# A hybrid decoder block on one core: the last unit's scores, the query remainder's buffer, and the last inverse deviation

## The chip, the cores and the metric

The kernel runs on one core of a Trainium2 chip. A core has TensorE (matrix products, "PE" in the profile, its weight loads "PEld"), VectorE ("DVE"), ScalarE ("ACT"), GpSimd ("POOL") and SyncE ("SP"), which here only issues DMAs. Each engine works through its own queue in order; the queues are tied to each other by semaphores. The metric is the time of one execution on the device in microseconds; of several runs the median is given.

## The reference

One decoder block over 512 tokens with 16 meta tokens put in front (L = 528 rows), model width 1024, in float32.

```python
h = layer_norm(concat(meta, x))
proj = h @ w_in                    # q, k, v, gate of both branches, two merge gates
# branch d: 8 heads, two score maps each, ALiBi, softmax; a = p0 - lam * p1; y_d = rms_norm(a @ v)
# branch s: 16 heads, stick-breaking:
z = q @ k.T * 64 ** -0.5
log_keep = where(before, log_sigmoid(-z), 0)
a = where(before, exp(log_sigmoid(z) + suffix_sum(log_keep)), 0)
y_s = a @ v
br_d = (y_d * silu(g_d)) @ w_br_diff
br_s = (y_s * silu(g_s)) @ w_br_sb
y = (sigmoid(m_d + b0) * br_d + sigmoid(m_s + b1) * br_s) @ w_out
out = layer_norm(2 ** 0.25 * h + y)[16:]
```

## The kernel before

**Precision.** Every large product is done in three: operands are split into a high part, rounded for the fast matmul form, and a remainder, and high times high, high times remainder and remainder times high are summed in PSUM. `hi` and `lo` (lines 176 to 192) split the weights, four blocks of 128 rows at a time ("a half"); the function `prep` does this four halves ahead of the use and fetches more weights. The remainders are subtractions on VectorE, the high parts casts on ACT.

**Units.** The attention runs in 16 units (`UNITS`): units 0 to 7 are the heads of branch d, units 8 to 15 are pairs of heads of branch s. While unit u does its scores, transposes and products with v, TensorE also projects the keys and values of unit u + 1 (`stage_kv`), the queries of unit u + 2 (`stage_q`) and a gate or two. In each unit the projections are generators that yield a time after each small step, and the function `run` (line 571) drives them; it holds a list of (time, work) pairs, the steps, and puts each piece of work out when the sum of the yielded times has passed its time. So the step times set the order in which instructions are written.

**What sets the order on the engines.** The written order is not yet the order of the queues. A planner simulates the program on a timeline at build time and draws up each engine's queue; it takes instructions that its simulation holds ready, earlier written ones first, and gives each tile one of the buffers of its ring as they come free. Where the kernel wants its own order it adds dependencies that need no semaphore: `keep_order` (line 235) ties each instruction of an engine to the one written before it. This is done for everything before the units, for all engines and SP from line 1027 on (the branch products, the output projection, the last LayerNorm), and, for TensorE alone, from a marker in the last unit on: the step at `LAST[0][0] - 0.1` (line 1022) stores the position, and line 1225 ties TensorE's instructions from there. Instructions written before the marker are free.

**A unit of branch s.** `s_scores` (line 892) does one head c of the pair: for the four blocks of 128 queries, from the last to the first, one or two score tiles (widths 264 and 264, 400, 272, 144), each two matmuls into a bank of the two called "sc" (line 756), two sigmoids on ACT (lines 902 and 904) which free that bank, then a scan and a product on VectorE (lines 908 and 909) which write the block of the weights a into the padded tile `apad`. It is a generator with five steps. `transposed` gives three parts that turn `apad` block by block on TensorE (line 768) into a bank of the two called "tp", and split what was turned (lines 773 and 774). `s_values` multiplies with v (lines 917 to 925) into the bank "av", and copies the result out (lines 929 to 933). `values` (line 720) prepares v: it turns vT into two "tp" banks, tv and t4, and splits them into V and v4 (lines 745 and 746, and line 747 for the last block); V has one buffer, so these casts follow the last product of the unit before.

**The last unit** (u = 15) has no keys or queries to project. Its projections are gate d, three merge gates and gate s, eight steps of 0.64 each. The scores of head 0 are put out at 0, 0.85, ..., 3.4, those of head 1 at 4.4, 5.25, 6.1, 6.95 and 7.8; the transposes of both at the times of `LAST`: 13.0, 14.1, 18.2 (with the product with v at 21.2) and 21.9, 21.9, 23.2 (24.9).

**The query remainder.** `stage_q` (line 606) scales the projected queries on ACT into A[0], takes the remainder on VectorE into the tile `low` (line 614) and sends three half tiles on by DMA (line 616). `low` comes from the ring "sg", six buffers of 128 x 512, which also serves the gates' sigmoids, the head outputs `ys`, and the reloads `gr` and `yd` of `late_gate` (lines 547 to 549). The tag "bias" of the pool `ap` has two buffers of 128 x 528; branch d keeps its biases there, and from unit 8 on one of them holds `diag`, a row mask for the scans.

**The end.** The output projection runs in two column halves c and four row blocks t (line 1188). In the second half each row block is finished: residual (line 1197), statistics (line 1200), their aggregation (line 1205), the inverse deviation by `rstd_of` (line 296: on GpSimd, an addition and a power of -0.5), then on VectorE `shift` (line 1210, subtract the mean and multiply by the weight) and `scale` (line 1214, multiply by the inverse deviation and add the bias), and the store. For the last row block the scaling and the store are done in two halves. ACT's last work is splitting `w_out` in the first column half (line 1131) and issuing two loads (line 1196).

Of the kernel before, what the change touches and what calls it, by code (L numbers as in the profile page):

```python
# [10 lines left out]
F32R = mybir.dt.float32r  # L11
BF16 = mybir.dt.bfloat16
AF = mybir.ActivationFunctionType
# [3 lines left out]
P = 128  # L17
D = 1024
KT = D // P
S = 512  # L20
M = 16
L = M + S
# [24 lines left out]
def hybrid_block_kernel(ctx: ExitStack, tc: tile.TileContext, x, meta, emb_g, emb_b, w_in, b_gate,  # L47
                        diff_lambda, subln_g, w_br_d, w_br_s, w_out, ln_g, ln_b, out):
    nc = tc.nc
    v, s, g, pe = nc.vector, nc.scalar, nc.gpsimd, nc.tensor  # L50
# [10 lines left out]
    gpool = ctx.enter_context(tc.tile_pool(name="g", bufs=6))  # L61
# [29 lines left out]
    for n, (kind, i) in enumerate(seq):  # L91
# [17 lines left out]
        else:  # L109
            c = COL[kind] + i * P  # L110
# [168 lines left out]
    epsr = const.tile([P, 1], F32, name="epsr")  # L279
# [16 lines left out]
    def rstd_of(pool, var, rs, n):  # L296
        e = pool.tile([P, 1], F32, tag="lne", name="lne")
        g.tensor_tensor(e[:n], var, epsr[:n], op=ALU.add)
        g.tensor_tensor(rs, e[:n], neghalf[:n], op=ALU.pow)
# [149 lines left out]
    def lam2():  # L449
        v.tensor_scalar(nlam, lexp[:, 1:2], lexp[:, 0:1], -LAM_INIT, op0=ALU.subtract, op1=ALU.add)  # L450

    steps = dict(a=scaled, d=lambda b, k: scaled(b, k, v), x=lambda b, k: query(0, P * b, P, k),
                 y=lambda h, k: query(1, 256 * h, 256, k), s=lambda h, k: high(h, k, s.copy),
                 h=lambda h, k: high(h, k, v.tensor_copy), l=low, N=norms, S=stat)
# [128 lines left out]
    with tc.tile_pool(name="att", bufs=1) as ap:  # L583
# [15 lines left out]
        diag, staged = [], []  # L599
# [6 lines left out]
        def stage_q(unit, kind, n):  # L606

            res = []
            yield from proj_tok(res, "q" + kind, n)
            ps = res[0]  # L610
            A = [apool.tile([P, S], F32R, tag=f"A{c}", name=f"A{c}") for c in range(2)]
            low = gpool.tile([P, S], F32R, tag="sg", name="low")
            s.activation(A[0], ps, AF.Copy, scale=0.125)
            v.scalar_tensor_tensor(low, ps, 0.125, A[0].bitcast(F32), op0=ALU.mult, op1=ALU.subtract)  # L614
            for o, src in ((A[1][LO], A[0][HI]), (A[1][HI], low[HI]), (A[0][HI], low[LO])):
                nc.sync.dma_start(o.bitcast(F32), src.bitcast(F32))
            unit["A"] = A
            yield 0.64
# [273 lines left out]
        def s_scores(unit, c, first):  # L892
            A = unit["A"]
            a = apads[c]
            sg, om = E
            for i in reversed(range(NB)):
                nk, z0 = NKEY[i], ZOFF[i]
                for n, (ps, k0, use) in enumerate(logits(A[c], K[c], i)):
                    if n == 1:
                        yield  # L900
                    o = ds(z0 + k0, use)
                    s.activation(om[:, o], ps[:, :use], AF.Sigmoid, scale=-1.0)  # L902
                    behind("act", first)
                    s.activation(sg[:, o], ps[:, :use], AF.Sigmoid)  # L904
                    behind("act", first)

                rev = om[:, z0:z0 + nk][:, ::-1]
                v.tensor_tensor_scan(rev, rev, diag[0][:, L - nk:][:, ::-1], 0.0, ALU.mult, ALU.max)  # L908
                v.tensor_tensor(a[:, ds(AOFF[i], nk - 1)], sg[:, ds(z0, nk - 1)], om[:, ds(z0 + 1, nk - 1)],
                                op=ALU.mult)  # L910
                yield
# [29 lines left out]
        def spread(gen, t0, dt, count):  # L941
            return [(t0 + dt * m, lambda: next(gen)) for m in range(count)]
# [12 lines left out]
        for u, (kind, n) in enumerate(UNITS):  # L955
            unit = units[u]
            if u + 3 == SEVEN:
                pools["rawk"] = ap
            last = u + 1 == len(UNITS)
            proj = [] if last else keys_values(units[u + 1], *UNITS[u + 1])  # L960
            if u + 2 < len(UNITS):
                proj.append(stage_q(units[u + 2], *UNITS[u + 2]))
            steps = pending + [(0.6, lambda unit=unit: values(unit, kind))]
            pending = []
            if u + 1 < SEVEN:
                steps.append((9.2, store_k))
            if u in SUMS_AT:
                if not tS:
                    tS.append(ypool.tile([P, KT, L], F32R, tag="ys", name="tS"))
                steps += [(t, lambda k=u + (u > 1) + m: placed(lambda: input_sums(k))) for m, t in enumerate(SUMS_AT[u])]  # L970
            if u in GATE_AT and u < 14:
                proj.append(raw_gate(GATE_AT[u], kept["r"][GATE_AT[u]]))
            if kind == "d":
                ta = {}
                dt, t0, t1 = TD[u in GATE_AT]
                steps += spread(d_scores(unit, n), 0.0, dt, 10)
                parts = transposed(ta, apads[n % 2])
                steps += [(t0 + 0.7 * m, f) for m, f in enumerate(parts)]
                steps.append((t1, lambda: d_values(unit, ta)))
                pending = [(3.0 if n < 7 else 5.8, lambda unit=unit, n=n: d_norm(unit, n))]  # L980
            else:
                if n == 0:
                    diag.append(ap.tile([P, L], F32, tag="bias", name="diag", bufs=2))
                    g.memset(diag[0], 0.0)
                    g.tensor_copy(diag[0][:, L - P:], ident)
                    g.memset(v3[:, 1], 0.0)
                    for a in apads:
                        for i in range(NB):
                            g.memset(a[:, ds(AOFF[i] + NKEY[i] - 1, 1)], 0.0)
                if last:  # L990
                    ydT = [pair_of("ydT", n=S) for k in range(4)]
                    ydT = [ydT[k % 4][:, k // 4, :] for k in range(8)]
                    ysT = ypool.tile([P, 8, S], F32, tag="ys", name="ysT")
                    ysT = [ysT[:, k, :] for k in range(8)]
                    unit["y"] = ysT[7]

                    def fill_in(y, of):
                        placed(lambda: nc.sync.dma_start(y, of), [mybir.EngineType.SP])

                    fill_in(ydT[7], kept["d"][7])  # L1000
                    for m, (y, of) in enumerate(((ydT, "gd"), (ysT, "gs"))):
                        for j in range(7):
                            steps.append((1.3 + 1.5 * (7 * m + j), lambda o=y[j], x=kept[of][j]: fill_in(o, x)))
                    proj += [gate("d", n, lambda: ydT[7]), merge_gate(0, 0), merge_gate(0, 1), merge_gate(0, 2),
                             gate("s", n, lambda: ysT[7])]
                else:
                    if GATE_AT.get(u) == n:
                        yd = gpool.tile([P, S], F32, tag="sg", name="yd")
                        nc.sync.dma_start(yd, kept["d"][n])
                        proj.append(gate("d", n, lambda yd=yd: yd, kept["gd"][n]))  # L1010
                    else:
                        steps += zip((12.0, 24.0), late_gate(ap, *(kept[x][n] for x in ("d", "r", "gd"))))
                    proj.append(gate("s", n, lambda unit=unit: unit["y"], kept["gs"][n]))
                for c in range(2):
                    ta = {}
                    steps += spread(s_scores(unit, c, n == 0), (2.0 + 4.3 * c) if n == 0 else 4.4 * c, 0.85, 5)
                    parts = transposed(ta, apads[c])
                    times = LAST[c] if last else [7.0 + 6.5 * c + 0.7 * m for m in range(3)] + [10.5 + 6.5 * c]
                    steps += zip(times, parts)
                    steps.append((times[3], lambda c=c, ta=ta: s_values(unit, c, n, ta)))  # L1020
                if last:
                    steps.append((LAST[0][0] - 0.1, lambda: state.update(ends=len(nc.cur_bb.bb.instructions))))
            run(proj, steps)
# [5 lines left out]
    lr = ctx.enter_context(tc.tile_pool(name="later", bufs=2))  # L1029
# [111 lines left out]
    for p in range(4):  # L1141
        steps = []
# [16 lines left out]
    def residual(t):  # L1159
        hr = hrs[t]  # L1160
        v.scalar_tensor_tensor(hr, hr, xmv[:, t, 0:1], vec["eg"], op0=ALU.subtract, op1=ALU.mult)
        v.scalar_tensor_tensor(hr, hr, xrs[:, t:t + 1], vec["eb"], op0=ALU.mult, op1=ALU.add)
# [4 lines left out]
    for k in range(5, KT):  # L1167
        split_out(0, k)
        if k == 5:
# [4 lines left out]
    MEANWHILE = [[lambda k=k: split_out(1, k) for k in range(3)] + [lambda: residual(0), lambda: load_rows(1)],  # L1174
                 [lambda k=k: split_out(1, k) for k in range(3, 6)] + [lambda: residual(1), lambda: load_rows(2)],
                 [lambda k=k: split_out(1, k) for k in range(6, 8)] + [lambda: residual(2), lambda: load_rows(3)],
                 [lambda: residual(3)], [], [], [], []]
    for c in range(2):
        for t in range(NB):
            st, final = sts[t], t == NB - 1  # L1180
# [22 lines left out]
            mv = lr.tile([P, 2], F32, tag="fmv", name="fmv")  # L1203
            rs = lr.tile([P, 1], F32, tag="frs", name="frs")
            v.bn_aggr(mv, st[:, :4 if final else 2])
            rstd_of(lr, mv[:, 1:2], rs, P)

            def shift(o, w, t=t, mv=mv):
                a = hrs[t][:, ds(o, w)]
# [46 lines left out]
```

## Time and profile before

| | us |
|---|---|
| median of 3 runs | 708.45 (708.07 to 708.89) |
| the profiled execution | 708.69 |
| its span, first to last instruction | 706.9 |
| the units, to the start of the branch products | 541.5 |
| branch products, gates and rounding to the first output product | 113.8 |
| output projection | 44.1 |
| behind the last matmul | 7.5 |

The granted TensorE clock was 0.998 of full speed over the span. The rows of the timeline give start and duration in microseconds, engine, line, operation, output from input, and in brackets how long the engine had been idle and what released it. A wait list gives, for an engine and a line, what it waited for: the sum, how often, and the longest. Matmuls are pipelined: they start 0.23 us (512 wide) or 0.12 us (264 wide) apart while each lasts longer, so starts are to be compared, not ends.

### The profile page before, as it was taken

To read this page: it belongs to the slowest core of one execution; us is meant where nothing else is said; L and a number is where in the kernel's file an instruction comes from. 1 tells how busy PE (TensorE), PEld (TensorE's weight loads), DVE (VectorE), ACT (ScalarE), POOL (GpSimd) and SP (SyncE) were. 2 spreads that over 40 slices of the span, in tenths; PEclk is the share of its full clock that TensorE was granted. 3 is DMA by queue.
4 is the path that set the end of the run, shared out by engine and by line. 5 is a ranking of instruction groups with operands and counts; after the bars stand their busy time and mean duration, and the time that the engine had idled before them with its cause. 6 is when DMAs were issued, how large, how long until landed. Compare 5 with 4: busy or idle time off the path is not lost.

```text
span 706.9 us, 13294 instructions
## 1 busy us (share of the span) xinstructions
PE 696.0 (98%) x4482; PEld 635.9 (90%) x4482; DVE 569.5 (81%) x1224; ACT 439.3 (62%) x1068; POOL 132.9 (19%) x146
## 2 busy tenths in 40 slices
PE   9999999999999999999999999999999999999995
PEld 8999999989989898988889899988888998999885
DVE  6887998878687687989787898966665888688886
ACT  5776768757566687776767687766555456555400
POOL 3243112322222101212123020000012201230012
PEclk9999999999999999999999999999999999999999
DMA  8398557988898886899897976645576749796702
GB/s 286 104 198 179 144 121 173 216 184 178 210 195 184 198 189 175 170 218 197 210 201 180 241 150 180 178 113 179 189 179 129 153 120 235 149 178 185 266 20 115
DMA packets 184054, 124.93 MB, mean 177 GB/s; under 512 B 8961, under 2 KB 168098, under 8 KB 183986
## 3 DMA queue, kind: packets, MB, share of 16 engines
q1 hardware_dynamic: 147890, 102.84, 50.0%
q0 software_dynamic: 35776, 20.19, 22.9%
q10 hardware_dynamic: 320, 1.06, 0.4%
q8 instruction: 35, 0.57, 0.4%
q14 instruction: 33, 0.27, 0.1%
HBM read 93.54 MB, written 9.44 MB: 146 GB/s over the span
## 4 chain that ended last, share of the span: by engine, by line
PE 91%; ACT 3%; issue 2%; DVE 1%; DMA 1%; POOL 0%; POOLq 0%; DVEq 0%; ACTq 0%
PE q L692 16%; PE ps L496 11%; PE ps L498 11%; PE ps L497 11%; PE q L1066 11%; PE pso L1188 6%; PE ps L512 6%; PE sc L756 5%; PE t L768 3%; PE bank L387 1%; PE warm L308 1%; PE tv L725 1%; DMA k<-ks 1%; PE av L923 1%; PE av L924 1%
## 5 line engine op out<-in xcount | busy, mean ns | idle before, releaser
L190 DVE TENSOR_TENSOR w<-raw,w 128x512 fp32r<-128x512 f32 x168 | 114.8, 689 | 40.3 <-ACT w L185 39.0
L496 PE MATMUL ps<-hTh,w 128*128 128x512 f32 x368 | 145.1, 394 | 0.0
L498 PE MATMUL ps<-hTh,w 128*128 128x512 f32 x368 | 144.8, 393 | 0.0
L497 PE MATMUL ps<-hTl,w 128*128 128x512 f32 x368 | 144.4, 393 | 0.0
L185 ACT CAST w<-raw 128x512 fp32r<-128x512 f32 x168 | 103.4, 627 | 13.7 <-PE ps L498 7.3
L147 POOL DMA_DIRECT2D rawk<-in_w_in_dram x48 | 66.1, 1631 | 118.8 <-DMA rawk<-in_w_in_dram 49.6
L692 PE MATMUL q<-tS,w 128*128 128x264 f32 x384 | 82.4, 291 | 0.0
L498 PEld LDWEIGHTS ps<-hTh,w 128*128 128x128 f32 x368 | 69.2, 188 | 13.8
L1066 PE MATMUL q<-gh,w 128*128 128x256 f32 x448 | 81.4, 284 | 0.2 <-ACT t L1075 0.2
L497 PEld LDWEIGHTS ps<-hTl,w 128*128 128x128 f32 x368 | 69.3, 188 | 12.9
L496 PEld LDWEIGHTS ps<-hTh,w 128*128 128x128 f32 x368 | 69.3, 188 | 12.7
L1066 PEld LDWEIGHTS q<-gh,w 128*128 128x128 f32 x448 | 70.2, 192 | 0.5 <-ACT t L1075 0.4
L756 PE MATMUL sc<-k,A 128*128 128x264 f32 (+3 forms) x320 | 65.4, 297 | 1.3 <-DMA k<-ks 1.0
L692 PEld LDWEIGHTS q<-tS,w 128*128 128x128 f32 x384 | 63.2, 189 | 1.1 <-DVE low L614 0.6
L1066 PE MATMUL q<-gl,w 128*128 128x256 f32 x224 | 63.5, 283 | 0.0
L692 PE MATMUL q<-hTh,w 128*128 128x264 f32 x288 | 61.2, 288 | 0.0
L908 DVE TENSOR_TENSOR_SCAN e<-e,diag 128x528 f32<-128x528 f32 (+1 forms) x64 | 53.7, 850 | 7.9 <-ACT e L902 7.7
L692 PE MATMUL q<-tl,w 128*128 128x264 f32 x192 | 55.0, 286 | 0.0
L756 PEld LDWEIGHTS sc<-k,A 128*128 128x128 f32 x320 | 50.2, 189 | 4.0 <-ACT e L904 1.9
L512 PE MATMUL ps<-hTh,w 128*128 128x264 f32 x256 | 51.6, 289 | 0.2 <-ACT k L634 0.2
L692 PEld LDWEIGHTS q<-hTh,w 128*128 128x128 f32 x288 | 47.7, 189 | 0.9 <-DVE kvt L712 0.2
L934 POOL DMA_DIRECT2D ys<-half x14 | 11.7, 837 | 193.3 <-ACT ys L933 163.7
(280 smaller groups left out, 1599.5 us busy)
## 6 DMA issues: line engine op xcount, KB each, us to landing
raw<-in_w_in_dram SPq DMA_DIRECT2D x140, 256.0 KB, 3.5
rawk<-in_w_in_dram POOLq DMA_DIRECT2D x48, 256.0 KB, 6.3
rawk<-in_w_in_dram SPq DMA_DIRECT2D x36, 256.0 KB, 3.6
k<-ks SPq DMA_DIRECT2D x60, 132.0 KB, 3.4
raw<-in_w_out_dram SPq DMA_DIRECT2D x16, 256.0 KB, 3.4
k<-ks SPq DMA_DIRECT2D x60, 66.0 KB, 3.2
A<-low SPq DMA_DIRECT2D x28, 128.0 KB, 3.0
raw<-in_w_br_diff_dram SPq DMA_DIRECT2D x12, 256.0 KB, 4.7
```

The lines of the kernel that those rows point to most:

```text
L147: second[l] = [lambda raw=raw, x=x: g.dma_start(raw, x, accum_op=ALU.add) for x in more]
L185: s.copy(wh, raw)
L190: eng.tensor_tensor(wl, raw, wh.bitcast(F32), op=ALU.subtract)
L496: pe.matmul(ps, wh[:, k % 4, :], hTh[:, k, M:], start=(k == 0), stop=False)
L497: pe.matmul(ps, wh[:, k % 4, :], hTl[:, k, M:], start=False, stop=False)
L498: pe.matmul(ps, wl[:, k % 4, :], hTh[:, k, M:], start=False, stop=(k == KT - 1))
L512: pe.matmul(ps[:, :H2], a[:, k % 4, :], b[:, k, ts(c, H2)], start=(k == 0 and m == 0), stop=(k == KT - 1 and m == 2))
L692: pe.matmul(bank, a[:, k, :], b, start=start and k == 0 and j == 0, stop=k == 3 and j == 2, skip_group_check=not start)
L756: pe.matmul(ps[:, :n], q, K[:, m, k0:k0 + n], start=(m == 0), stop=(m == 1))
L908: v.tensor_tensor_scan(rev, rev, diag[0][:, L - nk:][:, ::-1], 0.0, ALU.mult, ALU.max)
L1066: pe.matmul(bank, a[:, k, :], b[:, n, k, :], start=start and k == 0 and m == 0, stop=k == 3 and m == 2, skip_group_check=not start)
L1188: pe.matmul(ps, MH[k][:, ts(t, P)] if m == "h" else ML[:, k, ts(t, P)], WO[c]["hl".index(w)][:, k, r], start=(n == 0), stop=(n == 3 * KT - 1))
```

## The change

Three edits, with no change to what is computed except the way in which the last row block's inverse deviation is worked out.

In the last unit the last two of head 1's five score steps, the blocks of width 272 and 144, are put out at 13.6 and 15.0 instead of 6.95 and 7.8. That is behind the marker and, in the written order, behind the first and the second part of head 0's transposes, with one projection step between each.

From unit 8 on `low` is a fixed tile, made once from the tag "bias", which has a free buffer there; six of the fourteen remainders use it, those of units 10 to 15. The ring "sg" serves the rest as before.

For the last row block the inverse deviation is exp(-0.5 ln(var + eps)) in two ACT instructions instead of an addition and a power on GpSimd. The table set that has both functions is loaded by an instruction put out behind the matmuls of the second column half's first row block.

```diff
-            low = gpool.tile([P, S], F32R, tag="sg", name="low")
+            if diag:
+                if len(diag) == 1:
+                    diag.append(ap.tile([P, L], F32R, tag="bias", name="low", bufs=2))
+                low = diag[1][:, :S]
+            else:
+                low = gpool.tile([P, S], F32R, tag="sg", name="low")
...
-                    steps += spread(s_scores(unit, c, n == 0), (2.0 + 4.3 * c) if n == 0 else 4.4 * c, 0.85, 5)
+                    scores = spread(s_scores(unit, c, n == 0), (2.0 + 4.3 * c) if n == 0 else 4.4 * c, 0.85, 5)
+                    steps += scores[:3] + [(t, scores[0][1]) for t in (13.6, 15.0)] if last and c else scores
...
-                 [lambda: residual(3)], [], [], [], []]
+                 [lambda: residual(3)],
+                 [lambda: s.preload_act_table_set("natural_log_exp_and_others")], [], [], []]
...
-            rstd_of(lr, mv[:, 1:2], rs, P)
+            if final:
+                s.activation(rs, mv[:, 1:2], AF.Ln, bias=epsr)
+                s.activation(rs, rs, AF.Exp, scale=-0.5)
+            else:
+                rstd_of(lr, mv[:, 1:2], rs, P)
```

## The prediction

> **What bounds the kernel now.** I read the page's span and busy times first, then the waits of TensorE, then the chain of waits, then the timeline at the places that the diff touches.
>
> ```profile
> span 706.9 us, 13294 instructions
> ...
> PE 696.0 (98%) x4482; PEld 635.9 (90%) x4482; DVE 569.5 (81%) x1224; ACT 439.3 (62%) x1068; POOL 132.9 (19%) x146
> ```
>
> TensorE is busy in 98% of the span, so 706.9 - 696.0 = 10.9 us is all that any change of order can touch while the matmuls stay as they are. The diff adds and removes no matmul. Where the 10.9 us lie is told by the waits of TensorE (engine, line, what it waited for: sum, times, longest) and by its last matmul:
>
> ```profile
> PE sc L756 <- DMA k<-ks: 1.0, 1, 1.0
> PE sc L756 <- ACT e L904: 0.4, 1, 0.4
> ...
> 699.15 0.28 PE L1188 MATMUL pso<-wo1h,ml 128*128 128x256 f32 x1
> ```
>
> 706.9 - 699.43 = 7.5 us lie behind the last matmul. That leaves 3.4 us for the start and the whole middle. Two waits there touch the diff: one for keys (1.0 us) and one for an eviction of scores (0.4 us). The change therefore plays for two small sums: the tail, and these stalls.
>
> **The tail: ACT for the last inverse deviation.** The timeline behind the last matmul (start, duration, engine, line):
>
> ```profile
> 700.38 0.26 DVE L1205 BATCH_NORM_AGGREGATE fmv<-fst 128x2 f32<-128x24 f32 x1
> 700.68 1.31 DVE L1210 SCALAR_TENSOR_TENSOR hr<-hr,fmv,lgb 128x1024 f32<-128x1024 f32 x1
> 700.73 0.19 POOL L298 TENSOR_TENSOR lne<-fmv,epsr 128x1 f32<-128x1 f32 x1 [3.60 <-DVE fmv L1205]
> 700.99 1.40 POOL L299 TENSOR_TENSOR frs<-lne,neghalf 128x1 f32<-128x1 f32 x1
> 702.43 1.42 DVE L1214 SCALAR_TENSOR_TENSOR hr<-hr,frs,lgb 128x512 f32<-128x512 f32 x2 [0.44 <-POOL frs L299]
> ```
>
> VectorE ends its subtraction at 700.68 + 1.31 = 701.99 and could scale about 0.03 us later, the gap that it shows between two of its own instructions (fmv ends at 700.64, the next starts at 700.68). It scales at 702.43, because POOL's power ends only at 702.39. So 702.43 - 702.02 = 0.41 us can be had, and no more: below that the subtraction is itself the bound.
>
> What replaces POOL's two instructions is a logarithm and an exponential on ACT. The trace has no such pair on 128x1, so I bound it: from below by ACT's 128x1 scaling, from above by the same two functions on 128x512 (lines 883 and 885).
>
> ```profile
> L484 ACT ACTIVATE g<-cols 128x1 f32<-128x1 f32 x1 | 0.2, 204 | 0.0
> ...
> L883 ACT ACTIVATE r<-ms,epsr 128x512 f32<-128x512 f32 x8 | 5.6, 698 | 1.0 <-PE ms L878 1.0
> ...
> L885 ACT ACTIVATE r<-r 128x512 f32<-128x512 f32 x8 | 5.1, 642 | 0.1
> ```
>
> Start at 700.73, where POOL starts now, with the 0.07 us that POOL shows between its two instructions (700.92 to 700.99): the low bound ends at 700.73 + 0.20 + 0.07 + 0.20 = 701.20, the high one at 700.73 + 0.70 + 0.07 + 0.64 = 702.14. I take the low one, since its shape is the right one; then rs is ready 0.8 us before the subtraction ends, and the gain is the full 0.41. At the high bound it is still 702.43 - 702.16 = 0.27. Both output DMAs are issued behind that scaling, so the end moves with it. The three earlier row blocks keep POOL and are not on the path, since matmuls run beside them.
>
> The functions need their table. The diff puts the load in front, behind the matmuls of c = 1, t = 0. ACT's queue shows:
>
> ```profile
> 255.06 1.28 ACT L881 ACT_TABLE_LOAD   x1
> ...
> 667.84 0.44 ACTq L1196 DMA_DIRECT2D lgb<-in_ln_b_dram  x1
> ```
>
> The load takes 1.28 us, and ACT's last work before the tail is a DMA issue that ends at 668.28, 32 us before fmv. The load delays nobody: nothing is queued behind it but the new pair. If that cover were missing, it would cost 1.28 us on the path.
>
> The Trainium skill, "ScalarE: Activation LUTs", section "What ACT_TABLE_LOAD costs", speaks against such a move: it puts a switch of the table set at about 2.66 us, a load of 1283 ns and 1380 ns of draining. The trace agrees on the load (1.28); the row shows nothing of a drain. By either price the sum is unchanged as long as the load lies in those 32 us.
>
> **The last unit: two score blocks later.** Here is the stall that the change is aimed at, from the timeline of all engines, with one row of the groups of TensorE from 484.77 to the start of the branch products at 541.5 (three such rows, lines 496 to 498, have 75 each):
>
> ```profile
> 481.46 0.40 PE L925 MATMUL av<-al,V 128*128 128x512 f32 x1
> ...
> 483.13 0.48 ACT L745 CAST V<-tv 128x384 fp32r<-128x384 f32 x1
> ...
> 483.44 0.39 PE L497 MATMUL ps<-hTl,w 128*128 128x512 f32 x1
> ...
> 483.67 0.39 PE L498 MATMUL ps<-hTh,w 128*128 128x512 f32 x1
> ...
> 483.95 0.41 ACT L904 ACTIVATE e<-sc 128x264 f32<-128x264 f32 x1
> 484.12 0.28 DVE L746 TENSOR_TENSOR v<-t,v 128x128 fp32r<-128x128 f32 x1
> ...
> 484.41 0.52 PE L756 MATMUL sc<-k,A 128*128 128x272 f32 x2 [0.36 <-ACT e L904]
> ...
> 484.77 0.38 PE L768 MATMUL t<-ident,apad 128*128 128x128 f32 x2
> ...
> 485.69 0.32 ACT L747 COPY v<-tv 128x128 f32<-128x128 f32 x1
> ...
> 486.60 0.34 PE L756 MATMUL sc<-k,A 128*128 128x144 f32 x2
> ...
> L496 PE MATMUL ps<-hTh,w 128*128 128x512 f32 x75 | 29.7, 397 | 0.0
> ```
>
> Matmuls of this size follow each other every 0.23 us (483.44, 483.67), so TensorE is ready at 483.90 and starts the 272-wide block at 484.41: 0.51 us lost. It needs the score bank that ACT frees at 483.95 + 0.41 = 484.36. The diff takes that block out of the way, and the transposes (line 768) are next. But they need a bank of the two called "tp". One held tv, which is read until 485.69 + 0.32 = 486.01, after these transposes began; so they have the other, t4's, and t4 is read by VectorE until 484.12 + 0.28 = 484.40. **The new first in line is released 0.04 us later than the old one.** Both hang on the same chain: av at 481.46, ACT's two copies of it, its casts of V from 483.13, VectorE's remainder. All projection matmuls written before the transposes are used up by then (3 x 75 = 225 run behind 484.77: the 57 that the code writes after the transposes in this unit and 168 of the seven gates behind it), so none can fill the hole. The 0.51 us stay, and the two score blocks are done behind instead of in front: nothing. Bounds: a gain of 0.51 if the new plan frees the bank sooner, a loss of 486.01 - 484.41 = 1.60 if it gives the transposes tv's bank. I take 0, by the nearest row.
>
> What is late next? The 144-wide block comes a step of three matmuls (3 x 0.23 = 0.69 us) and a transposition later than now, some 1.1 us if that takes 0.4 (an estimate from the 0.36 between 484.41 and 484.77). Its product must be there for the transposes of the second half:
>
> ```profile
> 491.37 0.30 DVE L909 TENSOR_TENSOR apad<-e,e 128x143 f32<-128x143 f32 x1
> ...
> 497.26 0.60 PE L768 MATMUL t<-ident,apad 128*128 128x128 f32 x4
> ```
>
> From 491.67 to 497.26 there are 5.6 us, five times what is needed. The sigmoids of both blocks queue on ACT behind the cast of the transposed tile, the scans on VectorE likewise; weight preparation behind them runs four halves ahead.
>
> **The fixed tile.** Six query remainders (units 10 to 15) move from the ring "sg" of six buffers to a buffer of their own. No instruction, no byte and no DMA is added or removed. The own buffer is written once a unit and read by two DMAs that land long before the next unit's remainder, so it never waits. Does the ring cost anything today? The wait list of weight loads names the remainder:
>
> ```profile
> PEld q L692 <- DVE low L614: 0.6, 2, 0.3
> ```
>
> These two waits are for the projection's bank, which the remainder reads; the new tile doesn't free it sooner. By itself this part is worth 0. But instructions of this stage are ordered by a planner that counts free buffers, and with one buffer more in the ring it may draw another order for units 8 to 15. That can take away or add stalls of the kind seen once:
>
> ```profile
> 333.61 1.29 SPq L645 DMA_DIRECT2D k<-ks  x2
> ...
> 336.46 0.49 SPq L646 DMA_DIRECT2D k<-ks  x1
> ...
> 338.01 0.28 PE L692 MATMUL q<-hTh,w 128*128 128x264 f32 x1
> 338.13 0.40 PE L756 MATMUL sc<-k,A 128*128 128x264 f32 x2
> 339.49 0.48 PE L756 MATMUL sc<-k,A 128*128 128x264 f32 x2 [0.96 <-DMA k<-ks]
> ```
>
> Matmuls of this width start 0.12 us apart (338.01, 338.13); the second pair of scores starts 1.36 us after the first instead of 0.24, so 1.12 us is lost. A gain of at most 1.12, then, and a loss worked out below; I take 0, as the trace shows this wait once in all the units.
>
> **The sum.** -0.41 + 0 + 0 = -0.41 us. The profiled execution took 708.69 us, with a span of 706.9 and 1.8 around it; the median of the three runs shown is 708.45, so the same cut gives 708.04. **I predict 708.0 us.** About 0.2%, 1.4 us, is what a measurement of this kernel can tell from no change.
>
> **Rivals.**
> (a) *The late keys go too.* If the new order issues the third key piece (336.46) right behind its neighbours (ending 334.90), the scores no longer wait: 708.04 - 1.12 = 706.9; with the 0.51 us as well, 706.4. For it: one unit of the eight has the stall, so it is an accident of one order. Against: that order may stay as it is. Chance 0.25.
> (b) *Loads go ahead of the keys (slower).* A free ring buffer lets the planner issue the two reloads of a unit (lines 548 and 549) earlier, on SP's queue in front of the last key pieces.
>
> ```profile
> 304.44 0.59 SPq L646 DMA_DIRECT2D k<-ks  x1
> ...
> 307.75 0.65 PE L756 MATMUL sc<-k,A 128*128 128x264 f32 x4
> ...
> 339.43 0.50 SPq L548 DMA_DIRECT2D gr<-r  x1
> 339.97 0.42 SPq L549 DMA_DIRECT2D yd<-d  x1
> ...
> k<-ks SPq DMA_DIRECT2D x60, 66.0 KB, 3.2
> ```
>
> They hold the queue 0.50 + 0.42 = 0.92 us. The slack of the keys, by their 3.2 us to landing, is 307.75 - 304.44 - 3.2 = 0.11 in one unit and none in the unit at 338. Late in both: 0.81 + 0.92 = 1.73, and with a third unit at the lower price 2.54, so 708.04 + 2.54 = 710.6. It is a loss from one unit on, and shows as slower from two. Against it: at 339 the reloads stand behind all the keys. Chance 0.10.
> (c) *The transposes get tv's bank:* 708.04 + 1.60 = 709.6. Chance 0.08.
> (d) *The table doesn't hold,* and a load of 1.28 us stands in front of the logarithm: rs at 701.20 + 1.28 = 702.48, 0.09 after POOL's; the gain is gone and the time 708.5. Chance 0.07. In that case the skill's 1.38 us of draining, on the same page and section, would make it 709.9 by an estimate from its figure; no row here shows it.
>
> **How the numbers follow.** My forecast has 0.50. Within 0.2% lie the forecast, (c) and (d): 0.65. Faster by more is (a): 0.25; slower by more is (b): 0.10. The range from 706.6 to 709.8 leaves out (b) and the part of (a) with both stalls gone, 0.08: together 0.18.
>
> **What would show it.** In the tail: two ACT instructions of 128x1 that end before 701.99 as counted there, and VectorE's scaling within 0.05 us of its subtraction. Wrong is a table load beside them, or a pair longer than 1.2 us. In the last unit: the four transposes ahead of the 272-wide block, still about 0.5 us behind the last projection matmul, waiting for VectorE's v. No hole there, or one of 2 us, would make that step wrong. In units 8 to 15: the wait for keys once, about 1 us; two or more such waits, or none, is where the prediction would fail.

## The result and the profile after

| | before | changed |
|---|---|---|
| median of 21 runs each, us | 708.77 | 707.34 |
| range of the runs | 708.07 to 709.52 | 707.08 to 708.18 |
| span of the profiled execution | 706.9 | 705.6 |

The ratio is 0.9979, with a 95% interval of 0.9973 to 0.9985: 1.43 us faster, 0.2%, and clear of no change.

The page of the changed kernel, span and busy times:

```profile
span 705.6 us, 13287 instructions
...
PE 695.1 (99%) x4482; PEld 635.4 (90%) x4482; DVE 569.0 (81%) x1224; ACT 440.2 (62%) x1071; POOL 131.1 (19%) x144
```

The matmuls are the same 4482. ACT has three instructions more (the table load and the pair), POOL two less. Then what TensorE waited for, all of the answer (engine, line, what it waited for: sum, times, longest):

```profile
PE warm L308 <- POOL ident masks.py:199: 1.4, 1, 1.4
PE t L773 <- DVE v L751: 0.9, 1, 0.9
PE bank L341 <- ACT cols L412: 0.2, 1, 0.2
PE ps L512 <- ACT k L639: 0.2, 1, 0.2
PE q L1072 <- ACT t L1081: 0.2, 1, 0.2
```

Beside the list of before, two things are to be seen. The wait for keys (1.0 us) is gone, and so is one of 0.2 us of the transposes for VectorE's remainder (line 774 before). The wait in the last unit is still there, but twice as long, and it has changed its name: from the scores waiting for ACT's eviction to the transposes (line 773 here, 768 before) waiting for VectorE's remainder of v (line 751, 746 before). The timeline at that place:

```profile
479.98 0.40 PE L930 MATMUL av<-al,V 128*128 128x512 f32 x1
...
481.73 0.39 PE L498 MATMUL ps<-hTh,w 128*128 128x512 f32 x1
...
482.64 0.28 DVE L751 TENSOR_TENSOR v<-t,v 128x128 fp32r<-128x128 f32 x1
...
482.98 0.66 PE L773 MATMUL t<-ident,apad 128*128 128x128 f32 x4 [0.86 <-DVE v L751]
```

TensorE is ready at 481.73 + 0.23 = 481.96 and starts at 482.98: a hole of 1.02 us where before had 0.51. And the tail:

```profile
698.97 0.26 DVE L1212 BATCH_NORM_AGGREGATE fmv<-fst 128x2 f32<-128x24 f32 x1
699.27 1.28 DVE L1221 SCALAR_TENSOR_TENSOR hr<-hr,fmv,lgb 128x1024 f32<-128x1024 f32 x1
699.33 0.29 ACT L1214 ACTIVATE frs<-fmv,epsr 128x1 f32<-128x1 f32 x1 [31.81 <-DVE fmv L1212]
699.65 0.20 ACT L1215 ACTIVATE frs<-frs 128x1 f32<-128x1 f32 x1
700.67 1.42 DVE L1225 SCALAR_TENSOR_TENSOR hr<-hr,frs,lgb 128x512 f32<-128x512 f32 x2
```

From the start of the aggregation to that of the scaling 1.70 us pass, against 702.43 - 700.38 = 2.05 before: 0.35 us won.

Last, the place where the scores waited for keys, in the changed kernel: the last key store, the first scores, and, for the keys from 327 to 345 us, the time from issue to landing.

```profile
334.47 0.60 SPq L650 DMA_DIRECT2D k<-ks  x1
...
337.69 0.65 PE L761 MATMUL sc<-k,A 128*128 128x264 f32 x4
...
DMA to landing us min/median/max: 2.3/2.6/5.2
```

The four matmuls run in one piece now. The last key store is issued 3.2 us ahead of them; before it was 338.13 - 336.46 = 1.7 us.

TensorE's order parts from that of before at 278 us and meets it again in front of 488 us; the matmuls in between are the same. So the whole span can be added up from the starts, in the two profiled executions:

| stretch, us | before | changed | difference |
|---|---|---|---|
| to the last matmul ahead of the new order | 278.26 | 278.60 | +0.34 |
| from there to a matmul behind it | 211.53 | 209.75 | -1.78 |
| from there to the last matmul | 209.36 | 209.39 | +0.03 |
| last matmul to scaling | 3.28 | 2.93 | -0.35 |
| scaling to the end of the span | 4.49 | 4.96 | +0.47 |
| the span | 706.92 | 705.63 | -1.29 |

The first row is not of the change: it lies between 278.07 and 278.99 us in all the profiled executions here and below, and 0.5 us apart in two of the changed kernel. Without it the sum is -1.63 us, beside the 1.43 measured, whose interval is 1.1 to 1.9 us.

The second row holds three large holes, by the distance of starts beyond the usual 0.23 us (512 wide) and 0.12 us (264 wide):

| hole at | before | changed |
|---|---|---|
| 311 us (in front of transposes 0.38, behind a product with v 0.27) | 0.65 | 0 |
| 338 us (scores of unit 10) | 1.12 | 0 |
| last unit, in front of the first transposes or scores | 0.51 | 1.02 |

These give -1.26 us. The other 0.5 us lie in smaller gaps, of which the largest is 0.18 at 344 us. The first hole, in the kernel before (the last of the four score matmuls starts at 311.40):

```profile
310.92 0.77 PE L756 MATMUL sc<-k,A 128*128 128x400 f32 x4
311.91 0.55 PE L768 MATMUL t<-ident,apad 128*128 128x128 f32 x3 [0.22 <-DVE al L774]
312.21 0.48 PE L917 MATMUL av<-ah,V 128*128 128x512 f32 x1
312.71 0.39 PE L692 MATMUL q<-tS,w 128*128 128x264 f32 x1
```

The last row but one of the span is a loss that the prediction doesn't have: the 0.35 us won in front of the scaling are given back behind it. The output stores land later there, 2.4 us behind their issue instead of 2.0 (the kernel before first):

```profile
out_dram<-hr SPq DMA_DIRECT2D x2, 256.0 KB, 2.0
```

```profile
out_dram<-hr SPq DMA_DIRECT2D x2, 256.0 KB, 2.4
```

The stretch takes 4.48 or 4.49 us in the profiled executions of the kernel before and of the moved scores and ACT's part alone, and 4.95 to 5.17 in all nine of kernels with the fixed tile. So the loss comes with the tile. Its cause is open: in the nine a packet of an instruction queue falls into this stretch, in the three it doesn't, but no run tested whether that holds the store up. (The kernel with the reload's own buffer, below, has such a packet too, and 4.63 us.)

### The profile page after: what moved, and what is told of

Read it like the earlier page. It is cut to its first block, busy times and chain, and to the rows that moved or that the text cites. A ratio compares the mean times of both kernels' runs of the same rounds, so it can differ in the third digit from the quotient of the medians.

```text
span 705.6 us, 13287 instructions
## 1 busy us (share of the span) xinstructions
PE 695.1 (99%) x4482; PEld 635.4 (90%) x4482; DVE 569.0 (81%) x1224; ACT 440.2 (62%) x1071; POOL 131.1 (19%) x144
## 4 chain that ended last, share of the span: by engine, by line
PE 94%; ACT 2%; DVE 1%; issue 1%; DMA 1%; POOL 0%; DVEq 0%; SPq 0%; ACTq 0%; POOLq 0%
PE q L697 17%; PE ps L496 12%; PE ps L497 12%; PE ps L498 12%; PE q L1072 11%; PE pso L1195 6%; PE ps L512 6%; PE sc L761 6%; PE t L773 4%; PE bank L387 1%; PE tv L730 1%; PE av L928 1%; PE av L929 1%; DMA xt<-in_x_dram 1%; PE av L922 1%
## 5 line engine op out<-in xcount | busy, mean ns | idle before, releaser
L778 ACT CAST ah<-t 128x384 fp32r<-128x384 f32 (+2 forms) x72 | 34.4, 478 | 22.4 <-PE t L773 22.1
```

## The experiments

**One part at a time.** The theory after the result: the fixed tile saves nothing by itself, but gives the planner another order for units 8 to 15, and what was won in the middle is that order; the moved scores are worth 0. The rival: the moved scores, which were written to close the hole in the last unit, brought the gain.

The fixed tile alone:

```diff
+            if diag:
+                if len(diag) == 1:
+                    diag.append(ap.tile([P, L], F32R, tag="bias", name="low", bufs=2))
+                low = diag[1][:, :S]
...
```

> The fixed tile alone; scores and inverse deviation as before. Theory (the planner): the tile itself saves nothing, but the ring with one user less makes the planner draw another order for units 8 to 15, in which the wait for keys (1.12 us) and the hole near 311 us (about 0.5) are gone and the hole in the last unit grows from 0.5 to about 1.0. So 1.1 to 1.2 us less than before, ratio about 0.9984, no wait of TensorE for keys, and a wait of about 0.9 us for ACT's eviction in the last unit. Rival (the scores): what was won comes from the moved blocks, and this kernel takes the time of before, ratio 1.000, with the wait for keys still there or another in its place.

Measured: 707.75 us, ratio 0.9989 (0.9980 to 0.9998), 0.8 us. TensorE's waits of this kernel:

```profile
PE warm L308 <- POOL ident masks.py:199: 1.4, 1, 1.4
PE sc L761 <- ACT e L909: 0.8, 1, 0.8
...
```

No keys; the holes at 311 and 338 us are gone by the starts too, and the hole in the last unit measures 0.97, in front of the scores this time. TensorE's order is that of the changed kernel from 278 us to the last unit. The stretch of the new order takes 210.04 us, 1.49 less than before, with a hole of 0.26 at 402 us that the changed kernel's profiled execution hasn't; the end behind the scaling takes 5.05, 0.56 more. Together that is 0.93 us, and the timing's interval (0.1 to 1.4) takes in this and the forecast.

What the tile changes first is the place of the remainder itself. In unit 8, the row of ACT's copy A[0] and that of the remainder, before and then in the changed kernel:

```profile
266.10 0.63 ACT L613 ACTIVATE A<-ps 128x512 fp32r<-128x512 f32 x1
276.22 0.69 DVE L614 SCALAR_TENSOR_TENSOR low<-ps,A 128x512 fp32r<-128x512 f32 x1
```

```profile
266.44 0.63 ACT L618 ACTIVATE A<-ps 128x512 fp32r<-128x512 f32 x1
267.51 0.67 DVE L619 SCALAR_TENSOR_TENSOR low<-ps,A 128x512 fp32r<-128x512 f32 x1
```

From the end of the copy to the remainder 9.5 us pass before and 0.4 in the changed kernel. In the six units it is 5.7 to 10.4 us before, and 0.4 to 2.1 in the kernels with the tile. The ring did hold the remainder up, and with it the projection's bank that it reads. It shows as a late place in VectorE's queue, which other work filled.

The moved scores alone:

```diff
+                    steps += scores[:3] + [(t, scores[0][1]) for t in (13.6, 15.0)] if last and c else scores
```

> The two score blocks alone. Theory (the planner): 0 within 0.1 us, ratio 1.000. The hole of 0.5 us in the last unit stays, now before the transposes and waiting for VectorE's remainder of v instead of ACT's eviction; the wait for keys (about 1 us) stays. Rival (the scores): the hole of 0.51 us goes, ratio 0.9993 or less.

Measured: 708.86 us, ratio 1.0003 (0.9994 to 1.0011). The order of all engines is that of before up to the last unit. The timeline of TensorE there:

```profile
483.17 0.39 PE L497 MATMUL ps<-hTl,w 128*128 128x512 f32 x1
483.40 0.39 PE L498 MATMUL ps<-hTh,w 128*128 128x512 f32 x1
484.19 0.66 PE L768 MATMUL t<-ident,apad 128*128 128x128 f32 x4 [0.40 <-DVE v L746]
```

The scores are out of the way, and the transposes wait in their place: 484.19 - 483.63 = 0.56 us against 0.51. The rival falls.

ACT for the last inverse deviation alone:

```diff
+                 [lambda: s.preload_act_table_set("natural_log_exp_and_others")], [], [], []]
...
+            if final:
+                s.activation(rs, mv[:, 1:2], AF.Ln, bias=epsr)
+                s.activation(rs, rs, AF.Exp, scale=-0.5)
```

> ACT for the last inverse deviation alone. Theory: VectorE's scaling starts 0.3 to 0.4 us sooner after the last matmul, 2.93 us behind its start instead of 3.28; ratio about 0.9995; every matmul in the order of before, with both holes. Rival: the store's landing takes up what the scaling wins, ratio 1.000.

Measured: 708.25 us, ratio 0.9992 (0.9983 to 1.0001). The timing alone doesn't clear no change. The trace shows the scaling sooner:

```profile
701.00 0.26 DVE L1206 BATCH_NORM_AGGREGATE fmv<-fst 128x2 f32<-128x24 f32 x1
...
702.70 1.41 DVE L1219 SCALAR_TENSOR_TENSOR hr<-hr,frs,lgb 128x512 f32<-128x512 f32 x2
```

1.70 us once more, with every matmul in the order of before. From this scaling to the end of the span 4.48 us pass, against 4.49 before, so the store takes up nothing here and the rival falls.

The changed kernel with the scores put back to 6.95 and 7.8 (the tile and ACT):

> The changed kernel without the moved scores. Theory (the planner): as the changed kernel, about 1.4 to 1.5 us under before, ratio 0.9979, with the hole of about 1 us in the last unit, before the 272-wide scores instead of before the transposes. Rival (the scores): 0.5 us or more is given back, ratio 0.9986 or above.

Measured: 707.38 us, ratio 0.9980 (0.9972 to 0.9989), with a wait of 0.8 us in the last unit, in front of the scores. The moved scores can be left out without loss.

**What holds the transposes?** The theory says the bank of t4, free 3.0 us behind the start of the last product with v; whatever stands in front of the transposes until then is free. If so, moving the transposes, not the scores, closes the hole.

One projection step later (the marker, 0.1 ahead, moves along):

```diff
-LAST = [13.0, 14.1, 18.2, 21.2], [21.9, 21.9, 23.2, 24.9]
+LAST = [13.5, 14.1, 18.2, 21.2], [21.9, 21.9, 23.2, 24.9]
```

> The changed kernel with the first transposes of the last unit one projection step later (13.5 for 13.0), so that three matmuls stand in front of them. Theory (the bank): the transposes cannot start before the bank of t4 is free, 3.0 us behind the start of the last product with v of the unit before; whatever stands in front of them until then is free. The hole shrinks from 1.02 by 3 x 0.23 to about 0.33 us: 0.7 us under the changed kernel, ratio to before about 0.9969. Rival (the work behind sets the pace): a later first transposition makes the products with v late, the hole moves there, ratio 0.9979 as before or above.

Measured: 706.62 us, ratio 0.9978 (0.9969 to 0.9987). Two steps later, the scores behind them:

```diff
+LAST = [14.1, 14.8, 18.2, 21.2], [21.9, 21.9, 23.2, 24.9]
...
+                    steps += scores[:3] + [(t, scores[0][1]) for t in (14.2, 15.5)] if last and c else scores
```

> The changed kernel with the first transposes two projection steps later (14.1, the second part at 14.8, the two score blocks at 14.2 and 15.5). Theory (the bank): six matmuls (1.37 us) cover the hole of 1.02 us wholly, no wait of TensorE for VectorE's v is left, 1.0 us under the changed kernel, ratio to before about 0.9965. Rival (the work behind sets the pace): 0 or a loss.

Measured: 706.32 us, ratio 0.9973 (0.9962 to 0.9983). And the bank freed sooner, with the order of the splits turned round in the last unit alone (shortened):

```diff
-                for h, l, src in ((V...), (v4...)):
+                both = ((V...), (v4...))
+                for h, l, src in both[::-1] if unit is units[-1] else both:
```

> The changed kernel; in the last unit alone t4 is split ahead of tv, so that its bank is free sooner. Theory (the bank): VectorE reads t4 to its end about 0.7 us sooner, the hole shrinks from 1.02 to 0.3 to 0.5 us, ratio to before 0.9970 to 0.9973; the second part of the transposes may then wait up to 0.2 us for the other bank. Rival: the transposes hang on something else (their operand, ACT's work on the scores), the hole stays at 1.0 us and the ratio at 0.9979.

Measured: 706.87 us, ratio 0.9977 (0.9968 to 0.9986). TensorE in the last unit, first with one step, then with two, then with the splits turned round:

```profile
479.69 0.40 PE L930 MATMUL av<-al,V 128*128 128x512 f32 x1
...
482.12 0.39 PE L498 MATMUL ps<-hTh,w 128*128 128x512 f32 x1
482.68 0.66 PE L773 MATMUL t<-ident,apad 128*128 128x128 f32 x4 [0.18 <-DVE v L751]
```

```profile
482.70 0.40 PE L498 MATMUL ps<-hTh,w 128*128 128x512 f32 x1
482.93 0.60 PE L773 MATMUL t<-ident,apad 128*128 128x128 f32 x4
```

```profile
480.15 0.40 PE L931 MATMUL av<-al,V 128*128 128x512 f32 x1
...
481.90 0.39 PE L498 MATMUL ps<-hTh,w 128*128 128x512 f32 x1
482.46 0.66 PE L774 MATMUL t<-ident,apad 128*128 128x128 f32 x4 [0.18 <-DVE v L752]
```

With one step the transposes still start 482.68 - 479.69 = 2.99 us behind the product, as in the changed kernel (482.98 - 479.98 = 3.00); only what TensorE does in between has grown, and the hole is 0.33, as forecast. With two steps it is gone. With the splits turned round the 3.00 fall to 2.31, and the hole is 0.33 again. So the bank sets the start: shown from both sides. The ratios are another matter: with intervals of 0.0009 to either side they can't tell 0.7 us (0.001) from nothing, and those of one step and of the splits do not show it. The stretch of the new order does: 209.75 us in the changed kernel, 209.23 with one step, 209.24 with the splits and 208.61 with two steps. Closing the hole wholly is worth 1.1 us there; of the 0.7 us that one step and the splits take from it, 0.5 are left, as gaps behind it grow (with one step by 0.17 in front of the next transposes).

**The table.** Without the early load:

> The changed kernel without its early table load: a load stands in front of the logarithm and another in front of the exponential. Theory: the first has nothing to wait for and runs early, beside the matmuls; the second is on the path, 1.28 us, so that the inverse deviation is ready about 0.6 us behind the subtraction's end, and VectorE's scaling starts about 0.5 us later than in the changed kernel, 0.15 us later than with GpSimd: ratio to before about 0.9987. Rival: a load costs 2.66 us on the path (the Trainium skill, ScalarE: Activation LUTs, What ACT_TABLE_LOAD costs), and the scaling starts about 1.9 us later than in the changed kernel: ratio 1.0006.

Measured: 709.14 us, ratio 1.0010 (1.0001 to 1.0019): all that the change had won is lost, and more. The tail of this kernel:

```profile
698.42 0.26 DVE L1212 BATCH_NORM_AGGREGATE fmv<-fst 128x2 f32<-128x24 f32 x1
698.72 1.28 DVE L1221 SCALAR_TENSOR_TENSOR hr<-hr,fmv,lgb 128x1024 f32<-128x1024 f32 x1
698.76 1.28 ACT L1214 ACT_TABLE_LOAD   x1 [33.84 <-DVE fmv L1212]
700.06 0.29 ACT L1214 ACTIVATE frs<-fmv,epsr 128x1 f32<-128x1 f32 x1
700.37 1.28 ACT L1215 ACT_TABLE_LOAD   x1
701.67 0.20 ACT L1215 ACTIVATE frs<-frs 128x1 f32<-128x1 f32 x1
701.90 0.75 DVE L1225 SCALAR_TENSOR_TENSOR hr<-hr,frs,lgb 128x512 f32<-128x512 f32 x1 [1.90 <-ACT frs L1215]
```

Both my theory and the rival were off, the one in the count and the other in the price. There are two loads, one for each function, and the first is not early: ACT idles 33.84 us in front of it and is released by fmv, so in this program the load stands behind the wait for the logarithm's operand. Two loads of 1.28 us stand on the path, and the scaling comes 3.48 us behind the aggregation instead of 1.70: 1.78 us, and 2.2 by the ratios (0.0031). The Trainium skill, "ScalarE: Activation LUTs", section "What ACT_TABLE_LOAD costs", would have each switch cost about 2.66 us. The trace doesn't agree: the next instruction starts 0.02 us behind a load (698.76 + 1.28 to 700.06), and the second load 0.02 us behind the logarithm (700.06 + 0.29 to 700.37), so the draining part of that price is not seen.

**Is it the remainder, or only the order?** The kernel before, with another user taken out of the ring, the reload gr:

```diff
+            if len(diag) == 1:
+                diag.append(ap.tile([P, L], F32R, tag="bias", name="gr", bufs=2))
-            t.extend(gpool.tile([P, S], F32, tag="sg", name=x) for x in ("gr", "yd"))
+            t.extend([diag[1][:, :S], gpool.tile([P, S], F32, tag="sg", name="yd")])
```

> The kernel before, with one edit: not the query remainder but the reload gr of the late gates takes the free buffer of the tag bias; the remainder stays in the ring. Theory (the planner): any user taken out of the ring gives a new order for units 8 to 15; the order of the scores at 338 us differs here too, and the hole there and the one at 311 us change, with no say of the remainder's own buffer: the hole at 338 smaller than 0.5 us or gone, ratio between 0.9975 and 0.9995. Rival (the remainder itself holds something up): the holes at 311 and 338 us stay as in the kernel before and the ratio is 1.000.

Measured: 709.87 us, ratio 1.0014 (1.0004 to 1.0024): slower. Some of its waits of TensorE:

```profile
PE t L770 <- DVE al L776: 0.7, 1, 0.7
...
PE sc L758 <- DMA k<-ks: 0.4, 1, 0.4
...
PE av L919 <- ACT ys L935: 0.2, 1, 0.2
```

The one big hole at 338 us is gone here too; 0.28 us is left among those scores. But there is a hole of 0.5 us at 308 (for keys), and at 437 one of 1.3 us, mostly in front of transposes that wait for a split. The direction of my forecast was wrong.

The kernel is no blind draw of another order. What got the buffer moves forward, as the remainder did in the changed kernel: the reload of that unit is issued at 302.73 instead of 309.38, and so ahead of four pieces of the keys.

```profile
302.73 0.59 SPq L550 DMA_DIRECT2D gr<-r  x1
...
305.31 0.60 SPq L648 DMA_DIRECT2D k<-ks  x1
```

The last of these key pieces is issued at 305.31, where the kernel before has 304.44, and the scores at 308 wait for keys, with TensorE still in the order of before. That is rival (b) of the prediction, met in another kernel: a hole of 0.53 us, where 0.81 had been counted for this unit with two reloads in front. The remainder stays late here, 8.0 to 10.9 us behind ACT's copy. So an early remainder is not needed for the hole at 338 to go; whether the same thing took that hole away in both orders is not shown.

**The best version again,** beside the changed kernel on one chip. The changed kernel:

> The changed kernel once more, beside the next one on the same chip: ratio 0.9979 within 0.0008, the hole of 1.0 us in the last unit.

Measured: 707.27 us, ratio 0.9981 (0.9972 to 0.9989). The version with two steps:

> The version with the first transposes two projection steps later, once more: by the trace of its first run 1.0 us under the changed kernel (no hole in the last unit), so a ratio of 0.9965 where that has 0.9979; by the first timing 0.0006 under it only. Theory (the bank): the median lies 0.8 to 1.2 us under that of the changed kernel of this job. Rival: half of it is given back somewhere, 0.4 us.

Measured: 706.78 us, ratio 0.9969 (0.9956 to 0.9981). Its median is 0.5 us under that of the changed kernel beside it, its ratio 0.8 us; the two ratios of this version are 0.9973 and 0.9969. It is the fastest of the kernels run, though the intervals overlap. This profiled execution had no hole in the last unit, but one elsewhere:

```profile
402.67 0.40 PE L761 MATMUL sc<-k,A 128*128 128x264 f32 x2
403.86 0.48 PE L761 MATMUL sc<-k,A 128*128 128x264 f32 x2 [0.79 <-ACT e L909]
```

The same code, in the execution profiled first, had none there. By the starts it measures 0.95 us here. Nine profiled executions share TensorE's order at this place: this one, the tile alone with 0.26, and seven with none over 0.15. The changed kernel has the same order there, so the hole can come in it as well and is no measure of what separates the two.

## Why the prediction was right, and where it was not

The forecast was 708.0 us in a range of 706.6 to 709.8; 707.34 lies inside, but 0.7 us under the forecast and on the edge of what I had called no change.

*The tail:* predicted -0.41, shown -0.35 up to the scaling in each kernel with the edit and its early load. That mechanism held: the pair took 699.33 to 699.85, 0.52 us by the low bound's 0.47, and the subtraction became the bound. The term was mis-sized in its gap: I let VectorE follow its own subtraction by 0.03 us, and it took 700.67 - 700.55 = 0.12. "Both output DMAs are issued behind that scaling, so the end moves with it" held for ACT's part alone, and failed in the changed kernel, where the end came 0.47 us later behind the scaling. From the last matmul to the end of the span it has 2.93 + 4.96 = 7.89 us against 3.28 + 4.49 = 7.77.

*The moved scores:* predicted 0, with the hole kept and renamed. The run with this part alone shows just that, down to the releaser and to 0.01 us (0.04 more was forecast, and 0.51 became 0.56).

*The fixed tile:* "I take 0, as the trace shows this wait once in all the units" is the step that failed, and a few lines ahead of it "the new tile doesn't free it sooner". I had looked for the ring's price in the wait lists, which show no more of it than two waits of the weight loads (0.6 us): the planner had put the remainder late in VectorE's queue, 5.7 to 10.4 us behind the copy. With the tile it comes 0.4 to 2.1 us behind it, the bank is free that much sooner, and those two waits are gone. The redrawn order took away the hole at 338 us, my rival (a), and the one of 0.65 at 311, whose rows I had not looked for; it cost 0.5 us in the last unit, where two matmuls fewer were left behind the product with v to cover the same 3.0 us. With the smaller gaps that is -1.78 us, less 0.47 at the end of the span. Rival (a) was the case that came, without its second half. The total of 707.34 lies near the forecast partly by luck: this gain, the loss at the end and a smaller win in the tail stood against a forecast of the tail alone.

*The keys as the cause at 338:* I had read the row as late keys. In the three profiled executions that share that order (before, the scores alone, ACT alone) the hole is 1.12, 0.63 and 1.01 us, and its named releaser is the keys' DMA, then ACT's line 902, then 904. From 327 to 345 us the keys took this long from issue to landing, in the kernel before:

```profile
DMA to landing us min/median/max: 5.6/6.1/7.9
```

In the new order it is 2.6. Late keys and ACT's late eviction come together there; which of them alone would have kept the hole was not separated.

*The rivals not met:* in the changed kernel the reloads did not go in front of the keys (that needed a buffer for the reload), the transposes kept t4's bank, and the table held. The price of (d) was too low: without an early load there are two loads, not one.

## What to carry to other kernels

When an engine stalls in front of an instruction, look at what stands behind that instruction too: if the next one hangs on the same chain, moving the first only renames the wait, and what helps is other work in front of both, or a shorter chain. Where a planner draws the order, a shortage of buffers shows as a late place in a queue and not as a wait: compare when an instruction's operands are ready with when it runs. An edit that frees a buffer moves forward what gets it, and the new order is to be judged by its holes; a gain found so can be lost by the next edit. With the bounding engine at 98%, add up the whole span from the starts, and not only its large holes: here they left out 0.5 us won in small gaps and 0.47 lost behind the last matmul.

## What the runs showed of the hardware that was not expected

Without an early load, the table load in front of the logarithm came only with that instruction's operand, 33.84 us after ACT's last work. Two functions that one early load had served got a load each; a load took 1.28 us and the next instruction followed 0.02 us behind.

One order does not lose the same time in each execution: the hole at 338 us measured 0.63 to 1.12 us in three of one order, and the one at 402 us was there in two of nine.

VectorE's scaling, whose other operand came from ACT, started 0.11 to 0.12 us behind its own subtraction in all eight profiled executions with the pair and the early load, though that operand had been ready for 0.7 us (700.55 - 699.85 in the changed kernel).
